# A macaron block with fp32 matmuls by splits: sums of weights issued after the next splits, the first gate block copied out of its banks, the first norm's squares spread out, the plain block's pass scheduled later

## The chip, the core and the metric

The kernel runs on one core of a Trainium2 chip. The metric is the device time of one execution in microseconds. The engines are TensorE (PE: matmuls, with PEld for its weight loads), VectorE (DVE), ScalarE (ACT), GpSimd (POOL) and SyncE (SP, which here issues loads only).

## The reference, cut to what matters

256 tokens of width 2048 pass a half-step feed-forward, two mixers merged by gates, a second half-step feed-forward and a last norm. All data are float32.

```python
x = x + 0.5 * swiglu_ffn(rmsnorm(x, norm_ffn1_g), ffn1_w_gate, ffn1_w_up, ffn1_w_down)
h = rmsnorm(x, norm_mix_g)
proj = h @ w_in                       # 2048 x 11264: q, k, v, retention q, k, v, g, two gates
att = chunked_band_attention(...)     # 8 heads
ret = silu(g_r) * chunkwise_retention(rotary(q_r), rotary(k_r), v_r)
merged = sigmoid(gate_a) * (att @ w_out_att) + sigmoid(gate_r) * (ret @ w_out_ret)
x = x + merged @ w_out
x = x + 0.5 * swiglu_ffn(rmsnorm(x, norm_ffn2_g), ffn2_w_gate, ffn2_w_up, ffn2_w_down)
return rmsnorm(x, norm_final_g)

def swiglu_ffn(x, w_gate, w_up, w_down):      # 2048 -> 5632 -> 2048
    return (silu(x @ w_gate) * (x @ w_up)) @ w_down
```

## The kernel before, in words

**Products by splits.** A float32 product is made of three passes of a reduced format: every weight tile (128 x 2 x 512, two slices of the contraction) is split into a high half `hi` (a rounding copy on ScalarE, L129) and a low half `lo` (the difference, on VectorE, L130). `three` (L135 to L143) then issues hi times hi (L140), lo of the activations times hi (L141), and hi times lo of the weights (L143). The matmuls of L143 are the ones that need VectorE's `lo`.

**Steps.** All work of TensorE is a list `steps`, written out in order before anything is issued. A *standard* step multiplies one weight tile with both halves of the tokens: twelve matmuls. A step of a group (below) has six. `prep` of a step issues its split; `products` issues its matmuls. `run` goes through the list: at step c it first calls `prep_upto`, which issues the splits up to three steps ahead (four pairs of split tiles, `SPLIT_BUFS`), then the functions that are due at step c (`due`, filled by `later` and `at`), then the products of step c. Within an engine instructions run in the order in which they were issued.

**Groups.** Pairs of 512-column blocks, a gate block with its up block or two gate blocks of the mixer, are computed by a scheme of the Strassen kind: seven half products instead of eight, at the price of sums of weight tiles on VectorE. A group has four phases; r steps use weights as loaded, s steps use sums, and each kind has four steps per phase, numbered 0 to 3 (0r0, 0r1, 0s0, 0r2, 0s1, 0r3, 0s2, 0s3, then phases 1 and 2 alike, then 3s0 to 3s3). A group's tiles bear its first step's number: z10 is the first group of the first feed-forward, followed by z46, z82, up to z334; z392 to z543 are the mixer's five; z692, z728, z765, up to z1018 are those of the second feed-forward. The sums: in phase 0 `first` (L532) adds the kept tile to x behind the split of an r step (for steps 0 and 1 in the feed-forwards, where steps 2 and 3 are added by a transfer, `ADDED`; for all four in the mixer); in phase 1 the raw tile is added (L594) behind the split of an r step, and `third` (L580, L581) takes a difference and issues an accumulating load on POOL behind the split of an s step. 0s0 splits the x that `first` made for 0r0, and so on.

**Weaving.** `weave` puts standard steps of other jobs between the pairs of a group's steps, by shares. In a feed-forward these are the *plain* block's gate and up products (block 10, not in a group), and the passes of the down projection: first block 10's pass, then those of blocks 0 to 9. `at_hand` says from which step on a pass may come: for the plain block six steps after its up product ends. `put_mid` transposes and splits the activations of a block four steps after it is done.

**The start.** The first ten steps are the gate block of the plain pair (steps 0 to 7) and the first two of its up block. The group z10 follows from step 10. The gate block uses two banks of tag "z", of which there are three and which the groups use too; its Silu is put off by `GATE_WAIT` = 5 steps until the first norm is known, whose eight squares are issued two at a time at steps 8 to 11. Close by lie the sums of the normed activations (L486 to L500). At the end of the up product, `close` seeds the banks of the next pass (L791) around `up_done` (L758), which multiplies up with the gate.

Of the kernel before, what the change touches and what calls it, by code (L numbers as in the profile page):

```python
# [10 lines left out]
AF = mybir.ActivationFunctionType  # L11
# [4 lines left out]
P = 128  # L16
SEQ = 256
NT = SEQ // P
D = 2048
# [7 lines left out]
NB = 512  # L27
# [19 lines left out]
ADDED = (2, 3)  # L47
PLAIN = 10
PASSES = ((10,),) + tuple((b,) for b in range(10))
GATE_WAIT = 5  # L50
WARM = (6, 3)
TAIL_PARTS = ((0, slice(0, NB)), (1, slice(0, NB // 2)), (1, slice(NB // 2, NB)))

# [22 lines left out]
def block_kernel(ctx: ExitStack, tc: tile.TileContext, x, g1, w1g, w1u, w1d, gm, w_in, rel, woa, wor, wo,  # L76
                 g2, w2g, w2u, w2d, gf, cos, sin, decay, ident, out):
    nc = tc.nc
# [19 lines left out]
    def tmp_tile(name, tag="t", bufs=None):  # L98
        return tmp.tile([P, NB], F32, tag=tag, name=name, bufs=bufs)


    steps = []
    transfers = []
    kept = []
    state = {"dma": 0, "kept": 0, "prep": 0, "step": 0, "slots": SPLIT_BUFS}
    room = {"raw": RAW_BUFS, "kept": KEPT}
    due = {}

    def later(n, fn):
        due.setdefault(state["step"] + n, []).append(fn)  # L110

    def weights_tile(name):
        return wpool.tile([P, KC, NB], F32, tag="raw", bufs=RAW_BUFS, name=name)
# [111 lines left out]
    def load_some():  # L225
        while state["dma"] < len(transfers) and room["raw"]:
            room["raw"] -= 1
            transfers[state["dma"]]()
            state["dma"] += 1
        while state["kept"] < len(kept) and room["kept"] > 0 and kept[state["kept"]][0] <= state["step"]:  # L230
            room["kept"] -= 1
            kept[state["kept"]][1]()
            state["kept"] += 1

    def prep_upto(n):

        while state["prep"] < min(len(steps), n) and state["slots"]:
            s = steps[state["prep"]]
            load_some()
            state["slots"] -= 1  # L240
            s.prep()
            for ring in s.frees:
                room[ring] += 1
            state["prep"] += 1
        load_some()
# [270 lines left out]
    class Strassen:  # L516
# [50 lines left out]
        def step(self, phase, jc, of_sum):  # L567
            made = {}
            name = f"{self.name}{phase}{jc}{'rs'[of_sum]}"
            n = HALF_K // KC  # L570

            def load():
                made["raw"] = weights_tile(f"raw{name}")
                i = 2 - phase
                fetch(made["raw"], self.w[i], self.rows(1, jc), self.col[i])

            def third():

                x, k = self.x[jc], self.kept[jc]
                nc.vector.tensor_sub(k, x, k)  # L580
                nc.gpsimd.dma_start(x, chunk(self.w[0], self.rows(1, jc), self.col[0]), accum_op=ALU.add)  # L581

            def prep():
                x = self.x[jc]
                if not of_sum:
                    if phase == 0:
                        made["w"] = split(self.kept[jc], name)
                        if jc not in self.added:
                            self.first(jc)
                        return  # L590
                    raw = made.pop("raw")
                    made["w"] = split(raw, name)
                    if phase == 1:
                        nc.vector.tensor_add(x, x, raw)  # L594
                elif phase == 2:
                    made["w"] = split(self.kept.pop(jc), name)
                elif phase == 3:
                    made["w"] = split(self.x.pop(jc), name)
                else:
                    made["w"] = split(x, name)  # L600
                    if phase == 1:
                        third()

            bank, form, fresh, closing = {
# [4 lines left out]
            }[phase, of_sum]  # L609

            def products():
                hi, lo = made["w"]
                if fresh and jc == 0:
                    self.bank(bank)
                three([
                    (
                        self.acc[bank], self.norm.form(form, KC * jc + i), (hi[:, i, :], lo[:, i, :]),
                        fresh and jc == 0 and i == 0, closing and jc == n - 1 and i == KC - 1,
                    )
                    for i in range(KC)  # L620
                ], True)
                if jc == n - 1:
                    self.end(phase, of_sum)

            loaded = not of_sum and phase in (1, 2)
            frees = ["raw"] if loaded else ["kept"] if of_sum and phase > 1 else []
            return Step(self, 0, load if loaded else None, prep, frees, products)

        def end(self, phase, of_sum):
# [51 lines left out]
    def weave(jobs, apart, groups, lead, share, start=None, extra=0):  # L681


        queue = [(job, k) for job in jobs for k in range(0, job.nk, KC)]
        at_hand = {}

        def next_standard():

            if len(queue) <= apart:
                return False  # L690
            job, k = queue[0]
            if any(at_hand.get(b, len(steps) + 1) > len(steps) for b in job.needs):
                return False
            steps.append(standard(job, k))
            del queue[0]
            if job.makes is not None and k + KC == job.nk:
                at_hand[job.makes] = len(steps) + 6
            return True

        for _ in range(lead):  # L700
            next_standard()
        ends = []
        rate = (len(queue) - apart) / (len(groups) * sum(share))
        credit = 0.0
        first = max(len(steps) - 8, D // NB)
        for n, (b, make) in enumerate(groups.items()):
            group = make()
            loads = group.loads()
            if start is not None and n == 0:
                loads[0] = lambda load=loads[0]: [start(), load()]  # L710
            kept.extend((first + i if n == 0 else 0, fn) for i, fn in enumerate(loads))
            for i, part in enumerate(group.steps()):
                steps.extend(part)
                credit += rate * share[i]
                if i + 1 == len(share):
                    at_hand[b] = len(steps) + 7

                turn = i + 1 == 3 * (HALF_K // KC)
                if (turn or credit >= (0.2 if (i + 1) % (HALF_K // KC) == 0 else 0.6)) and next_standard():
                    credit -= 1  # L720
            ends.append(len(steps))
        if extra:
            due.setdefault(ends[0], []).append(lambda: room.update(kept=room["kept"] + extra))
            due.setdefault(ends[-1], []).append(lambda: room.update(kept=room["kept"] - extra))
        for job, k in queue:
            steps.append(standard(job, k))

    def ffn(name, norm, wg, wu, wd, after, start=None):
# [10 lines left out]
        def plain(b):  # L739
            gates = {}  # L740

            wait = GATE_WAIT if start is not None and b == PLAIN else 0

            def gate_done(acc):
                def go():
                    for t in range(NT):
                        gates[t] = tmp_tile(f"{name}g{b}{t}", "gate", 2)
                        nc.scalar.activation(gates[t], acc[t], AF.Silu, scale=norm.scale(t))

                if wait:  # L750
                    later(wait, go)
                else:
                    go()

            def up_done(acc):
                for t in range(NT):
                    a = gates[t]
                    nc.vector.scalar_tensor_tensor(a, acc[t], norm.scale(t), a, op0=ALU.mult, op1=ALU.mult)  # L758
                later(4, lambda: put_mid(b, gates))

            tags = ("acc", "acc")
            up = Gemm(wu, 0, b * NB, D // P, norm, up_done, tags)
            up.makes = b
            return [Gemm(wg, 0, b * NB, D // P, norm, gate_done, ("z", "z") if wait else tags), up]

        def paired(b):
            got = {}
# [46 lines left out]
    n1 = Norm("n1", gains[:, 0, :], True)  # L814
# [13 lines left out]
    scale = HD ** -0.5  # L828
# [316 lines left out]
    def at(step, fn):  # L1145
        due.setdefault(step, []).append(fn)
# [40 lines left out]

    for c in range(2, 2 * (D // NB)):
        at(c - 1, lambda c=c: n1.put(c // 2, c % 2))
    for b in range(D // NB):  # L1190
        at(D // NB * 2 + b, lambda b=b: [n1.square(b, t) for t in range(NT)])
    at(60, load_angles)

    def set_bias():
# [77 lines left out]
```

## Time and profile before

| | |
|---|---|
| median of 3 runs | 2061.39 us (2060.89 to 2062.56) |
| the profiled execution | 2061.97 us, its span 2060.1 us |
| mean granted TensorE clock | 0.998 |
| TensorE busy | 2037.8 us (99%), 9208 matmuls |
| VectorE busy | 1766.2 us (86%) |
| ScalarE busy | 1494.1 us (73%) |
| POOL busy | 344.8 us (17%) |
| bytes moved | 498.47 MB, mean 242 GB/s |

A row of the timeline reads: start, duration (both us), engine, line, operation, output <- inputs, shapes, count, and in brackets the idle time before it with what ended that. A row of the list of waits reads: who waited, for whom, us in total, how often, the longest. Names such as loz29801r mean: the low half for group z298, phase 0, tile 1, an r step. Durations of neighbouring rows overlap a little, since an instruction starts before the one ahead of it has fully ended; times from start to start are what an engine needs for each.

### The profile page before, as it was taken

The page shows a single profiled execution, that of the slowest core. Times are in us where ns is not written, and L with a number is a line of the kernel's source. Part 1 is how long each engine was busy: PE and PEld are TensorE (multiplying, and loading weights), DVE is VectorE, ACT ScalarE, POOL GpSimd, SP SyncE. Part 2 cuts the span into 40 slices and gives each one's busy share as a digit, 9 for nine tenths or more (in the row PEclk, how much of TensorE's full clock was granted, in tenths as well). Part 3 has the DMA queues.
Part 4 walks back from the last instruction along what each step waited for, and adds up shares of the span by engine and source line. Part 5 has one row for each costly group of instructions (what it writes and reads, how often), then busy time and mean ns, then how long its engine had stood idle before and what let it go on. Part 6 is the DMA issues. An engine that isn't in the chain of part 4 may idle for free.

```text
span 2060.1 us, 26318 instructions
## 1 busy us (share of the span) xinstructions
PE 2037.8 (99%) x9208; PEld 1685.6 (82%) x9208; DVE 1766.2 (86%) x1836; ACT 1494.1 (73%) x1892; POOL 344.8 (17%) x386
## 2 busy tenths in 40 slices
PE   9999999999999999999999999999999999999998
PEld 7888888888888888888888888888888888888886
DVE  7999999999999799889966667569989999989996
ACT  8778877887877767776765434556788888887875
POOL 2221222221222110121100000012122212112200
PEclk9999999999999999999999999999999999999999
DMA  9888899888888677898786645578889888889983
GB/s 308 252 232 260 252 274 273 254 229 252 254 250 244 241 206 262 263 288 240 228 277 184 216 142 189 185 231 218 267 267 278 255 255 234 269 261 268 276 214 133
DMA packets 230325, 498.47 MB, mean 242 GB/s; under 512 B 15584, under 2 KB 16336, under 8 KB 230192
## 3 DMA queue, kind: packets, MB, share of 16 engines
q1 hardware_dynamic: 156736, 301.50, 43.5%
q0 software_dynamic: 70112, 189.44, 36.0%
q10 hardware_dynamic: 3344, 5.84, 0.8%
q8 instruction: 72, 1.18, 0.2%
q14 instruction: 61, 0.50, 0.1%
HBM read 487.81 MB, written 8.91 MB: 241 GB/s over the span
## 4 chain that ended last, share of the span: by engine, by line
PE 92%; ACT 3%; DVE 3%; issue 1%; DMA 1%; DVEq 0%; ACTq 0%; POOLq 0%; POOL 0%
PE acc L143 15%; PE acc L140 15%; PE acc L141 15%; DVE lo L130 1%; DMA raw<-in_w_in_dram 1%; ACT hi L129 0%; PE z392a L143 0%; PE z873a L140 0%; PE z910a L141 0%; PE z765a L141 0%; PE z543a L143 0%; PE z430a L143 0%; PE z801a L143 0%; PE z392a L141 0%; PE z505a L143 0%
## 5 line engine op out<-in xcount | busy, mean ns | idle before, releaser
L130 DVE TENSOR_TENSOR lo<-raw,hi 128x1024 fp32r<-128x1024 f32 x367 | 447.1, 1221 | 142.6 <-ACT hi L129 140.8
L129 ACT CAST hi<-raw 128x1024 fp32r<-128x1024 f32 x367 | 384.3, 1051 | 173.3 <-PE acc L141 138.0
L794 ACT ACTIVATE xall<-acc 128x512 f32<-128x512 f32 x160 | 94.5, 591 | 14.5 <-PE acc L143 10.3
L791 ACT ACTIVATE acc<-xall 128x512 f32<-128x512 f32 x160 | 95.8, 599 | 8.2 <-DVE f1g L758 4.3
L140 PE MATMUL acc<-hi,mgh 128*128 128x512 f32 x128 | 50.2, 392 | 0.0
L141 PE MATMUL acc<-hi,mgl 128*128 128x512 f32 x128 | 49.8, 389 | 0.0
L140 PE MATMUL acc<-hi,nma01h 128*128 128x512 f32 x96 | 38.8, 404 | 0.1
L140 PE MATMUL acc<-hi,nma00h 128*128 128x512 f32 x96 | 38.6, 402 | 0.0
L141 PE MATMUL acc<-hi,nma00l 128*128 128x512 f32 x96 | 37.5, 390 | 0.0
L141 PE MATMUL acc<-hi,nma01l 128*128 128x512 f32 x96 | 37.5, 390 | 0.0
L140 PE MATMUL acc<-hi,nma10h 128*128 128x512 f32 x96 | 37.5, 390 | 0.0
L141 PE MATMUL acc<-hi,nma11l 128*128 128x512 f32 x96 | 37.4, 390 | 0.0
L140 PE MATMUL acc<-hi,nma11h 128*128 128x512 f32 x96 | 37.4, 390 | 0.0
L141 PE MATMUL acc<-hi,nma10l 128*128 128x512 f32 x96 | 37.4, 390 | 0.0
L143 PE MATMUL acc<-lo,mgh 128*128 128x512 f32 x128 | 35.5, 389 | 0.0
L143 PE MATMUL acc<-lo,nma01h 128*128 128x512 f32 x96 | 29.6, 390 | 0.0
L143 PE MATMUL acc<-lo,nma11h 128*128 128x512 f32 x96 | 29.6, 389 | 0.0
L143 PE MATMUL acc<-lo,nma00h 128*128 128x512 f32 x96 | 29.6, 389 | 0.0
L143 PE MATMUL acc<-lo,nma10h 128*128 128x512 f32 x96 | 29.6, 389 | 0.0
L143 PEld LDWEIGHTS acc<-lo,mgh 128*128 128x128 f32 x128 | 24.0, 188 | 5.0
L141 PEld LDWEIGHTS acc<-hi,mgl 128*128 128x128 f32 x128 | 24.0, 188 | 4.9
L140 PEld LDWEIGHTS acc<-hi,mgh 128*128 128x128 f32 x128 | 24.0, 188 | 4.8
(6634 smaller groups left out, 7134.3 us busy)
## 6 DMA issues: line engine op xcount, KB each, us to landing
raw<-in_ffn_w_down_dram SPq DMA_DIRECT2D x176, 512.0 KB, 7.6
raw<-in_w_in_dram SPq DMA_DIRECT2D x96, 512.0 KB, 4.7
raw<-in_w_out_dram SPq DMA_DIRECT2D x32, 512.0 KB, 4.1
raw<-in_ffn_w_up_dram SPq DMA_DIRECT2D x16, 512.0 KB, 6.4
raw<-in_w_out_att_dram SPq DMA_DIRECT2D x16, 512.0 KB, 4.3
raw<-in_w_out_ret_dram SPq DMA_DIRECT2D x16, 512.0 KB, 3.9
raw<-in_ffn_w_gate_dram SPq DMA_DIRECT2D x15, 512.0 KB, 4.8
z392x<-in_w_in_dram POOLq DMA_DIRECT2D x8, 512.0 KB, 7.5
```

Source lines behind the costliest of these rows:

```text
L129: nc.scalar.copy(hi, raw)
L130: nc.vector.tensor_sub(lo, raw, hi.bitcast(F32))
L140: nc.tensor.matmul(acc, ahi, whi, start=first, stop=False, **more)
L141: nc.tensor.matmul(acc, alo, whi, start=False, stop=False, **more)
L143: nc.tensor.matmul(acc, ahi, wlo, start=False, stop=last, **more)
L791: nc.scalar.activation(acc, xs[t][:, cols], AF.Copy, scale=2.0)
L794: nc.scalar.activation(xs[t][:, cols], acc, AF.Copy, scale=0.5)
```

## The change

- The sums are put off: `soon(n, fn)` keeps a function until n further splits have been issued. `first` and the phase 1 addition of r steps go behind the next split, `third` behind the second next. The raw tile of a phase 1 r step is counted as free only when its addition has been issued.
- The plain block's pass may come nine steps after its up product instead of six. Written out, the list of steps changes in two groups only. In z10 the two standard steps of that pass leave phase 2 (behind 2r2 and 2s3) and stand behind 2s3 and 3s2. In z728 the phase 0 order 0r0, 0r1, standard, 0s0, 0r2, standard, 0s1, 0r3, 0s2, 0s3, standard becomes 0r0, 0r1, 0s0, 0r2, 0s1, 0r3, standard, 0s2, 0s3, standard, and phases 1 and 2 are shifted by one standard step.
- The first gate block uses the banks of tag "acc"; ScalarE copies it unscaled into two tiles of another ring when it is done, and the Silu, with the norm's scale, runs on these in place, twelve steps later.
- The eight squares of the first norm are issued one at a step at steps 10 to 17.

```diff
-GATE_WAIT = 5
+GATE_WAIT = 12
+SQUARES = 10
...
+    postponed = []
+
+    def soon(n, fn):
+        postponed.append([n, fn])
...
             load_some()
             state["slots"] -= 1
+            waiting = list(postponed)
             s.prep()
+            for p in waiting:
+                p[0] -= 1
+                if p[0] == 0:
+                    p[1]()
+                    postponed.remove(p)
             for ring in s.frees:
                 room[ring] += 1
...
                         if jc not in self.added:
-                            self.first(jc)
+                            soon(1, lambda: self.first(jc))
                         return
                     raw = made.pop("raw")
                     made["w"] = split(raw, name)
                     if phase == 1:
-                        nc.vector.tensor_add(x, x, raw)
+
+                        def second():
+                            nc.vector.tensor_add(x, x, raw)
+                            room["raw"] += 1
+
+                        soon(1, second)
...
                     if phase == 1:
-                        third()
+                        soon(2, third)
...
-            frees = ["raw"] if loaded else ["kept"] if of_sum and phase > 1 else []
+            frees = ["raw"] if loaded and phase == 2 else ["kept"] if of_sum and phase > 1 else []
...
             if job.makes is not None and k + KC == job.nk:
-                at_hand[job.makes] = len(steps) + 6
+                at_hand[job.makes] = len(steps) + 9
...
             def gate_done(acc):
-                def go():
+                for t in range(NT):
+                    gates[t] = tmp_tile(f"{name}g{b}{t}", *(("qk", 4) if wait else ("gate", 2)))
+
+                def go(srcs):
                     for t in range(NT):
-                        gates[t] = tmp_tile(f"{name}g{b}{t}", "gate", 2)
-                        nc.scalar.activation(gates[t], acc[t], AF.Silu, scale=norm.scale(t))
+                        nc.scalar.activation(gates[t], srcs[t], AF.Silu, scale=norm.scale(t))
 
                 if wait:
-                    later(wait, go)
+                    for t in range(NT):
+                        nc.scalar.copy(gates[t], acc[t])
+                    later(wait, lambda: go(gates))
                 else:
-                    go()
+                    go(acc)
...
-            return [Gemm(wg, 0, b * NB, D // P, norm, gate_done, ("z", "z") if wait else tags), up]
+            return [Gemm(wg, 0, b * NB, D // P, norm, gate_done, tags), up]
...
-    for b in range(D // NB):
-        at(D // NB * 2 + b, lambda b=b: [n1.square(b, t) for t in range(NT)])
+    for i in range(NT * D // NB):
+        at(SQUARES + i, lambda i=i: n1.square(i // NT, i % NT))
```

## The prediction

> **What bounds the kernel now.** I read the busy times of the page first, then the list of TensorE's waits, then the timeline around each of these waits and around the same places where nothing waits.
>
> ```profile
> PE 2037.8 (99%) x9208; PEld 1685.6 (82%) x9208; DVE 1766.2 (86%) x1836; ACT 1494.1 (73%) x1892; POOL 344.8 (17%) x386
> ...
> L130 DVE TENSOR_TENSOR lo<-raw,hi 128x1024 fp32r<-128x1024 f32 x367 | 447.1, 1221 | 142.6 <-ACT hi L129 140.8
> ```
>
> TensorE is the bound at 99%, VectorE stands close behind at 86%. So only TensorE's waits can be won, and an edit that makes VectorE late anywhere is paid in full.
>
> ```profile
> PE acc L143 <- DVE lo L130: 4.9, 9, 0.6
> PE z10c L140 <- ACT f1g L748: 2.2, 1, 2.2
> PE acc L141 <- DVE f2a10l L380: 1.4, 1, 1.4
> ...
> PE z1018c L143 <- DVE loz101800s L130: 0.6, 1, 0.6
> PE z982c L143 <- DVE loz98200s L130: 0.5, 1, 0.5
> ...
> PE acc L141 <- DVE f1a10l L380: 0.5, 1, 0.5
> ```
>
> These are what the change aims at: a low half that comes late in nine group starts of the first feed-forward and two of the second (z982, z1018), the bank of the gate block (z10c), and the plain block's pass (f1a10, f2a10). All other group starts of the second feed-forward and of the mixer wait for nothing now, so they can only lose.
>
> **Part 1: the sums put off, where a standard step follows.** The steps of a first-feed-forward group begin 0r0, 0r1, standard, 0s0 (r: kept weights, s: the sums). The timeline of group z298:
>
> ```profile
> 534.97 1.22 DVE L130 TENSOR_TENSOR loz29800r<-z298k,hiz29800r 128x1024 fp32r<-128x1024 f32 x1
> 535.63 1.04 ACT L129 CAST hiz29801r<-z298k 128x1024 fp32r<-128x1024 f32 x1
> 536.11 1.22 DVE L532 TENSOR_TENSOR z298x<-z298x,z298k 128x1024 f32<-128x1024 f32 x1
> ...
> 539.14 0.39 PE L140 MATMUL acc<-hi,f1a6h 128*128 128x512 f32 x1
> 539.51 1.22 DVE L130 TENSOR_TENSOR lo<-raw,hi 128x1024 fp32r<-128x1024 f32 x1
> 540.79 0.73 PE L143 MATMUL acc<-lo,f1a6h 128*128 128x512 f32 x2 [0.58 <-DVE lo L130]
> 541.36 0.40 PE L140 MATMUL acc<-hi,f1a6h 128*128 128x512 f32 x1
> ```
>
> VectorE runs lo r0, sum 0, lo r1, sum 1, lo standard, each 1.13 us behind the last (534.97, 536.11). Six matmuls take 1.36 us at 0.227 from start to start; from 539.14 to 541.36 they took 2.22, so the wait costs 0.86, more than its 0.58. After the change the order is lo r0, lo r1, sum 0, lo standard, sum 1, lo s0. Lo r1 now stands directly behind lo r0, but its high half is only there at 535.63 + 1.04 = 536.67: lo r1 starts at 536.72, the sum at 537.86, lo standard at 538.99 instead of 539.51. Gain 0.52, not 0.86. Lo s0 then ends near 542.5, some 0.5 before it is needed, so no new wait. Eight groups (z82 to z334): -4.2 us, between -6.9 (all 0.86) and 0.
>
> **Part 1 where no standard step follows.** Seven of the later groups begin 0r0, 0r1, 0s0, 0r2. The timeline of z801, which does not wait now:
>
> ```profile
> 1579.83 1.22 DVE L130 TENSOR_TENSOR loz80100r<-z801k,hiz80100r 128x1024 fp32r<-128x1024 f32 x1
> 1580.49 1.04 ACT L129 CAST hiz80101r<-z801k 128x1024 fp32r<-128x1024 f32 x1
> 1580.97 1.22 DVE L532 TENSOR_TENSOR z801x<-z801x,z801k 128x1024 f32<-128x1024 f32 x1
> 1582.30 1.06 ACT L129 CAST hiz80100s<-z801x 128x1024 fp32r<-128x1024 f32 x1 [0.77 <-DVE z801x L532]
> 1584.37 1.22 DVE L130 TENSOR_TENSOR loz80100s<-z801x,hiz80100s 128x1024 fp32r<-128x1024 f32 x1
> 1585.51 1.22 DVE L130 TENSOR_TENSOR loz80102r<-z801k,hiz80102r 128x1024 fp32r<-128x1024 f32 x1
> 1586.32 0.61 PE L143 MATMUL z801c<-loz80100s,n2s5h 128*128 128x512 f32 x2
> 1587.68 0.62 PE L143 MATMUL z801a<-loz80102r,n2a00h 128*128 128x512 f32 x2
> ```
>
> Step s0 splits the sum itself: its high half on ScalarE waits for sum 0 (the row at 1582.30), its low half for that. Now sum 1 fills this time on VectorE. After the change sum 0 starts behind lo r1: high half of r1 ends 1581.53, lo r1 1581.57, sum 0 1582.7 to 1583.9, high half of s0 1584.0 to 1585.1, lo s0 1585.15, and VectorE stands still for 1.2 us because sum 1 is queued behind lo s0. Then sum 1 at 1586.3, lo r2 at 1587.4 to 1588.6 instead of 1585.51. TensorE wants it with its weight load 0.23 before 1587.68: some 1.2 us late, and no later wait takes that back. z837 has the same rows (+1.2). In z765 sum 1 delays the last combination that the next transposes need, by the same 1.13 (+1.25). In z910 and z946 a standard step between the groups leaves room: 0. In z982 (z1018 alike) there is nothing in hand:
>
> ```profile
> 1888.28 1.04 ACT L129 CAST hiz98201r<-z982k 128x1024 fp32r<-128x1024 f32 x1
> 1892.17 1.22 DVE L130 TENSOR_TENSOR loz98200s<-z982x,hiz98200s 128x1024 fp32r<-128x1024 f32 x1
> 1894.93 0.62 PE L143 MATMUL z982a<-loz98202r,n2a00h 128*128 128x512 f32 x2
> ```
>
> The same walk from 1889.36 (lo r1) gives lo s0 at 1892.9 and lo r2 done at 1896.4, against 1894.70 for its weight load: +1.7 each, so the 0.5 us waits grow to over 2.
>
> The mixer's z430 has this order too, and sums in all four steps:
>
> ```profile
> 790.90 1.05 ACT L129 CAST hiz43001r<-z430k 128x1024 fp32r<-128x1024 f32 x1 [0.45 <-ACT z392c L1041]
> 797.62 0.62 PE L143 MATMUL z430a<-loz43002r,nma00h 128*128 128x512 f32 x2
> ```
>
> Lo r1 at 792.0, sum 0 to 794.35, lo s0 795.55, lo r2 done at 799.05 against 797.4: +1.6; z392 (r3 and s3 without a standard step between) +0.3, z543 +0.1. Mixer together +2.0, between 0 and +3.
>
> **Part 1 in the second phase.** Every sum there follows its split one or two places later, but standard steps lie between, so each low half has as many or fewer instructions ahead of it than now: 0. The raw buffer comes free one VectorE instruction (1.13 us) later, and SP's next load with it; POOL's accumulating loads shift by two to three. A whole phase of eight steps (eight times 1.36 us) hides both; if it did not, a late raw tile would stop ScalarE's split and cost its lateness in full.
>
> **Part 2: the plain block's pass, three steps later.** In the first feed-forward the pass goes to the end of phase 2; that is in part 3's sum. In the second, group z728 loses its first standard step and becomes 0r0, 0r1, 0s0, 0r2, 0s1, 0r3.
>
> ```profile
> 1455.52 1.04 ACT L129 CAST hiz72801r<-z728k 128x1024 fp32r<-128x1024 f32 x1
> ```
>
> The f2a10l wait goes (1.7 with its restart). But the walk from 1456.6 gives the high half of s0 at 1460.05 for a step due at 1459.5, and behind lo s0 (to 1461.3), sum 1 and two low halves of the plain block, lo r2 ends at 1464.8, 2.2 us late. Ahead of the pass the steps stand some 1.5 us later than now: +1.5, between -1.7 (the wait goes, nothing comes) and +3.
>
> **Part 3: the gate block, the squares, the first group.**
>
> ```profile
> 33.82 1.06 ACT L129 CAST hiz1001r<-z10k 128x1024 fp32r<-128x1024 f32 x1 [1.38 <-PE acc L141]
> 34.91 1.23 DVE L130 TENSOR_TENSOR loz1001r<-z10k,hiz1001r 128x1024 fp32r<-128x1024 f32 x1 [0.22 <-ACT hiz1001r L129]
> 47.31 0.50 PE L140 MATMUL z10c<-hiz1000s,n1s5h 128*128 128x512 f32 x1 [2.19 <-ACT f1g L748]
> 47.95 0.63 PE L140 MATMUL z10c<-hiz1000s,n1s5h 128*128 128x512 f32 x1
> 48.38 0.63 PE L141 MATMUL z10c<-hiz1000s,n1s5l 128*128 128x512 f32 x1
> 54.74 0.57 ACT L634 COPY z10b<-z10a 128x512 f32<-128x512 f32 x1 [0.77 <-PE z10a L143]
> ...
> 78.82 1.22 DVE L580 TENSOR_TENSOR z10k<-z10x,z10k 128x1024 f32<-128x1024 f32 x1
> 81.09 1.40 DVE L758 SCALAR_TENSOR_TENSOR f1g<-acc,n1rstd,f1g 128x512 f32<-128x512 f32 x2
> 81.87 0.60 ACT L791 ACTIVATE acc<-xall 128x512 f32<-128x512 f32 x1 [4.29 <-DVE f1g L758]
> ```
>
> And VectorE's busy time in two stretches, from the first sum to phase 1 and from there to the end of the f1g product:
>
> ```profile
> 34.00:57.77 23.77, 20.83 (x27) 0.93 0.73 213
> 57.77:82.49 24.72, 24.72 (x23) 1.00 0.84 223
> ```
>
> The z10c wait goes: 2.3 us and 1.7 more, since the next nine matmuls start 0.43 apart (47.95, 48.38; the granted clock of that stretch is 0.93) instead of 0.227. Two copies of 0.57 (the price of row 54.74) come in; the second delays the split of 33.82 by about 1. Lo r1 starts at 35.9 instead of 34.91, with sum 0 still behind it: VectorE is 2.1 us back. It was idle for 2.9 us in the first stretch, so it only just catches up by the start of phase 1; in the second stretch it was never idle. TensorE comes 4 us early and has to wait for it. Squares, table load and Silu, now near 57 to 60, hold ScalarE another 0.5 to 1 us. One put-off difference (as at 78.82) passes behind the f1g product, which so ends near 81.9, 0.6 earlier; the transposes and the second half of phase 2 hang on it. There eight steps without a standard one ask for VectorE every 1.36 us while it has the put-off difference, two low halves and a combination to fit in. I get the start of z46 about 1 us later than now, less its own 0.86 wait that the late pass removes: +0.1 instead of -5.6, between -4 and +2.
>
> **Sum.** -4.2 + 2.0 + (1.25 + 1.2 + 1.2 + 1.7 + 1.7) + 1.5 + 0.1 = +6.4 us. The profiled execution took 2061.97 us (span 2060.1), 0.6 above the median 2061.39 of the runs; on the median this is 2067.8, 0.3% slower.
>
> **Rivals.**
> The clock falls at the new waits. Row 47.31: a wait of 2.19 halved the rate of nine matmuls (1.7 us); the f2a10l wait of 1.4 did not, since the span lost there was the wait alone. My longest new waits are 2.2 (z728) and 1.6 (ahead of the f1a10 transposes). If two of them pay, 2071.2.
> [...]
> The first group keeps its 4 us, VectorE catching up where I see it bound: 2063.7, no change. For it: the 2.9 us of gaps before phase 1, which more than the 2.1 could fill; against: none from there to 82.49.
> Faster: the waits go and nothing comes. That is 4.0 (z10c) + 0.7 (f1a10) + 9 x 0.86 + 2 x 0.84 + 1.7 = 15.8 us: 2045.6. It is decided by one thing, whether s0's high half still starts before TensorE needs it; it would hold if ScalarE had r1's high half at least 1.2 us earlier. Row 1582.30, a split that waits for the sum already, speaks against it. With half of that gain and half of my costs (10.5) it is -7.9 + 5.3: 2058.8, the low end of the range.
>
> **How the numbers follow.** About 0.2% (4.1 us) is what a measurement here can tell from none. My sum 0.48 (2065 to 2071), the clock falling as well 0.12, the first group's gain kept 0.26, faster 0.14. Slower 0.60, same 0.26, faster 0.14. The range 2058 to 2073 leaves out most of the last case and the far end of the second.
>
> **What would show it.** Right: the L143 wait of the f1 starts at 0.1 to 0.3 instead of 0.58; ScalarE's s0 split in z801 waiting for L532 until about 3.5 us behind r1's split, and TensorE waiting for lo of 0r2 there and in z837, z982, z1018, z430; the z10c wait gone, but the f1a10 transposes still near 82. Wrong: z801 to z837 without a wait, or f1a10 transposes at 80.

## The result, and the profile after

The changed kernel takes 2076.41 us (median of 4 runs, 2074.92 to 2077.41) against 2061.14 before: a ratio of 1.0072 (95% interval 1.006 to 1.0084), 15.3 us slower where +6.4 was forecast. Its profiled execution has a span of 2075.1 us, 15.0 more, at the same mean clock of 0.998. The diff moves line numbers: L129, L130 and L140 to L143 of before are L134, L135 and L145 to L148 here, `first` is L543, the second sum L607, `third` L591 and L592.

The busy times and the chain of work that ended last, from the page of after:

```profile
PE 2048.4 (99%) x9208; PEld 1681.8 (81%) x9208; DVE 1769.9 (85%) x1836; ACT 1476.0 (71%) x1894; POOL 344.5 (17%) x386
...
PE 80%; DMA 6%; ACT 5%; issue 4%; DVE 4%; POOL 1%; ACTq 0%; DVEq 0%; POOLq 0%
PE acc L145 14%; PE acc L146 14%; PE acc L148 14%; DMA z190x<-in_ffn_w_gate_dram 1%; DMA z837x<-in_ffn_w_gate_dram 1%; ACT hi L134 1%; DMA z154x<-in_ffn_w_gate_dram 1%; DMA z298x<-in_ffn_w_gate_dram 1%; DMA z801k<-in_ffn_w_up_dram 1%; DMA z46x<-in_ffn_w_up_dram 0%; DMA z298x<-in_ffn_w_up_dram 0%; DVE lo L135 0%; ACT xall L814 0%; DMA z46k<-in_ffn_w_up_dram 0%; DMA z154x<-in_ffn_w_up_dram 0%
```

The same shares in the page of before:

```profile
PE 92%; ACT 3%; DVE 3%; issue 1%; DMA 1%; DVEq 0%; ACTq 0%; POOLq 0%; POOL 0%
```

TensorE is still "busy" for 99%, which tells nothing. The chain does: transfers (DMA) hold 6% of it, where they held 1%, and the largest of these are x tiles of groups of the feed-forwards. The list of TensorE's waits of after, the two waits of the start and of the mixer's norm left out:

```profile
PE z10c L145 <- ACT z10s L653: 2.7, 1, 2.7
PE z728a L148 <- DVE loz72802r L135: 1.6, 1, 1.6
...
PE z298c L145 <- ACT z298s L653: 1.0, 1, 1.0
...
PE z1018c L145 <- ACT hiz101800s L134: 0.9, 1, 0.9
PE z982c L145 <- ACT hiz98200s L134: 0.9, 1, 0.9
...
PE z801a L148 <- DVE loz80102r L135: 0.6, 1, 0.6
PE z837a L148 <- DVE loz83702r L135: 0.6, 1, 0.6
...
PE z430a L148 <- DVE loz43002r L135: 0.6, 1, 0.6
```

The row "acc <- lo, 9 times" of before is gone, and z728, z801, z837, z982, z1018 and z430 wait for the low halves that the prediction named (z982 and z1018 also for the high half of 0s0). Two kinds of row it did not have: z10c waiting 2.7 us for ScalarE's L653, and the same line in z298 (and, at 0.2 to 0.5, in z46, z118, z154 and z190). L653 is ScalarE's scaled copy of bank c; step 1r0 writes into bank c again and must wait for it.

Where the time went is read best by the start of each group. The table gives the start of a group's first matmul in the timeline of a kernel, less its start in before (us; the last column is step 3s3 of z1018). Column to column it shows the first group, the first feed-forward's groups, the mixer, z728, and the rest.

| kernel | z46 | z392 | z692 | z765 | z873 | end |
|---|---|---|---|---|---|---|
| changed | +1.0 | +5.4 | +7.1 | +8.7 | +11.8 | +15.1 |
| e1 first sums alone | -0.2 | -5.0 | -2.3 | -0.1 | +3.0 | +6.2 |
| e2 second sums alone | -0.1 | +1.0 | +3.1 | +3.1 | +3.1 | +3.0 |
| e3 third sums alone | -0.9 | +7.5 | +7.0 | +7.0 | +7.0 | +10.5 |
| e4 gate block and squares alone | -1.9 | -1.6 | -2.1 | -2.1 | -2.1 | -2.1 |
| e5 changed, third sums at once | +0.9 | -4.2 | +0.4 | +1.9 | +5.0 | +8.2 |
| e6 e3 with early loads | -0.4 | -0.3 | -0.7 | -0.8 | -0.8 | -0.8 |
| e7 later pass alone | +0.9 | 0.0 | -0.4 | -0.8 | -0.8 | -0.8 |
| e10 changed with early loads | +1.1 | -4.1 | -2.0 | -0.5 | +2.6 | +5.8 |

Each row is one profiled execution: that of e2 was 1.5 us slower than the median of its runs, that of e5 1.9 faster. The profiled execution of before lost 0.4 us in the mixer's z467, where a raw tile came late; all kernels but e2 and e5 are without that loss, so in their rows 0.4 us of what stands from z692 on is not an effect of the edit.

As an example of the rows behind the table, the first matmul of z298 in before, after and e10, in this order:

```profile
536.42 0.39 PE L140 MATMUL z298a<-hiz29800r,n1a00h 128*128 128x512 f32 x1
```

```profile
539.92 0.39 PE L145 MATMUL z298a<-hiz29800r,n1a00h 128*128 128x512 f32 x1
```

```profile
533.38 0.39 PE L145 MATMUL z298a<-hiz29800r,n1a00h 128*128 128x512 f32 x1
```

The changed kernel loses 4.4 us between z46 and z392, where the prediction had it win 4.2. The rest of the table's first row is near the forecast. So there was one thing to find: what the nine groups of the first feed-forward pay.

**The chain behind it in z298.** POOL's loads for z298, first in before, then in after (L581 and L592: the accumulating loads that `third` issues; L543 and L554: tiles of the next group; L547 and L558: the accumulate onto two of its x tiles; in brackets the idle time ahead):

```profile
515.01 1.20 POOL L581 DMA_DIRECT2D z262x<-in_ffn_w_up_dram  x1 [1.54 <-ACT hiz26221r L129]
...
521.77 0.73 POOL L543 DMA_DIRECT2D z298x<-in_ffn_w_gate_dram  x1 [1.90 <-DVE loz26221s L130]
533.49 1.23 POOL L547 DMA_DIRECT2D z298x<-in_ffn_w_up_dram  x1 [10.98 <-DMA z298x<-in_ffn_w_gate_dram]
537.40 1.21 POOL L547 DMA_DIRECT2D z298x<-in_ffn_w_up_dram  x1 [2.68 <-DMA z298x<-in_ffn_w_gate_dram]
...
547.48 1.06 ACT L129 CAST hiz29803s<-z298x 128x1024 fp32r<-128x1024 f32 x1 [0.30 <-PE z298c L141]
```

```profile
522.48 1.20 POOL L592 DMA_DIRECT2D z262x<-in_ffn_w_up_dram  x1 [2.19 <-ACT hiz26220s L134]
...
525.41 1.20 POOL L554 DMA_DIRECT2D z298x<-in_ffn_w_gate_dram  x1
...
526.96 1.08 POOL L554 DMA_DIRECT2D z298x<-in_ffn_w_gate_dram  x1
541.37 1.24 POOL L558 DMA_DIRECT2D z298x<-in_ffn_w_up_dram  x1 [13.32 <-DMA z298x<-in_ffn_w_gate_dram]
544.83 1.22 POOL L558 DMA_DIRECT2D z298x<-in_ffn_w_up_dram  x1 [2.23 <-DMA z298x<-in_ffn_w_gate_dram]
...
554.19 1.05 ACT L134 CAST hiz29803s<-z298x 128x1024 fp32r<-128x1024 f32 x1 [4.09 <-DMA z298x<-in_ffn_w_up_dram]
...
560.65 0.69 ACT L653 ACTIVATE z298s<-z298c,n1minus 128x512 f32<-128x512 f32 x1
561.39 0.50 PE L145 MATMUL z298c<-hiz29810r,n1s3h 128*128 128x512 f32 x1 [1.01 <-ACT z298s L653]
```

Read each against the start of z298 (536.42 and 539.92). The last accumulating load of z262 goes out 21.4 us ahead of it before, 17.4 after: 4.0 later. Six loads of z298 stand behind it on POOL. By the trace's times of landing they come in one behind the other, 1.6 to 2.1 us apart in both kernels, so the last of them, which goes out 13.0 us ahead of the start instead of 14.7, lands 4.6 behind it instead of 0.7. The accumulate onto the fourth x tile must wait until that tile has landed, and is issued 4.9 us behind the start instead of 1.0. From issue to landing it then takes 9.3 us instead of 6.2, so that its data are there 14.2 us behind the start instead of 7.2. In before the split of 0s3 came 11.1 us behind the start: the data had been there for 3.9 us, and its wait of 0.30 was for a free split tile. In after it waits 4.09 us for the data, everything behind it on ScalarE is late, L653 too, and TensorE waits at 1r0.

That is about half of the loss. By steps, the nine groups from z46 to z334 of after win 5.2 us at their starts, between 0r0 and 0s3, as e5 and e10 do. Then they lose 4.4 between 0s3 and 1s3, nearly all of it at 1r0 and 1r1, and 5.2 more in phase 2, at waits too short for the list. In z298 the second part shows at 2r1: the low half on VectorE and TensorE's matmul with it in after, then the low half in e10, whose start is 533.38.

```profile
584.48 1.22 DVE L135 TENSOR_TENSOR loz29821r<-rawz29821r,hiz29821r 128x1024 fp32r<-128x1024 f32 x1
585.75 0.73 PE L148 MATMUL z298b<-loz29821r,n1a01h 128*128 128x512 f32 x2
```

```profile
575.03 1.22 DVE L135 TENSOR_TENSOR loz29821r<-rawz29821r,hiz29821r 128x1024 fp32r<-128x1024 f32 x1
```

Against the start of z298 this low half begins at 44.6 us in after and at 41.7 in e10, with the same order of sums. VectorE had to wait for the late high half of 0s3 too and has been 2.9 us behind since, while TensorE has lost only 1.4 by then; so the low half comes late for it, 0.3 us at 2r1 and again at 2r3. Why z82 loses nothing and z262 only 0.4 stays open.

**The first group.** ScalarE and TensorE of after around 1r0 of z10, then TensorE at the same place in the best version (e8):

```profile
56.84 1.05 ACT L134 CAST hiz1011r<-rawz1011r 128x1024 fp32r<-128x1024 f32 x1
57.90 1.28 ACT L766 ACT_TABLE_LOAD   x1
59.20 1.33 ACT L766 ACTIVATE f1g<-f1g,n1rstd 128x512 f32<-128x512 f32 x2
60.44 0.67 ACT L653 ACTIVATE z10s<-z10c,n1minus 128x512 f32<-128x512 f32 x1
...
61.16 0.80 PE L145 MATMUL z10c<-hiz1010r,n1s3h 128*128 128x512 f32 x1 [2.67 <-ACT z10s L653]
61.75 0.63 PE L146 MATMUL z10c<-hiz1010r,n1s3l 128*128 128x512 f32 x1
62.18 0.63 PE L145 MATMUL z10c<-hiz1010r,n1s3h 128*128 128x512 f32 x1
```

```profile
60.47 0.50 PE L145 MATMUL z10c<-hiz1010r,n1s3h 128*128 128x512 f32 x1 [2.67 <-ACT z10s L651]
60.81 0.39 PE L146 MATMUL z10c<-hiz1010r,n1s3l 128*128 128x512 f32 x1
61.04 0.40 PE L145 MATMUL z10c<-hiz1010r,n1s3h 128*128 128x512 f32 x1
```

The bank wait of before is gone and z10 runs 4.3 us early from 0s1 on. But the put-off Silu with its table load stands directly ahead of L653 on ScalarE: 2.54 us from 57.90 to 60.44, and TensorE waits 2.67. Behind that wait the next matmuls of after start 0.43 apart instead of 0.23, so that of the 4.3 us 1.5 are left at 1r0 and 0.1 at 1r1. The busy times and the granted clock (third from the right) of after in the two stretches that the prediction quoted show the slow clock moved from one to the other:

```profile
34.00:57.77 23.77, 23.77 (x107) 19.68 (x106) 21.20 (x27) 20.93 (x36) 3.19 (x3) 1.00 0.75 204
57.77:82.49 24.72, 22.05 (x91) 17.79 (x90) 23.33 (x22) 15.32 (x18) 3.61 (x3) 0.93 0.77 207
```

### The profile page after: what moved, and what is told of

It reads as the page before. It is cut to its first block, busy times and chain, and to the rows that moved or that the text cites. A ratio compares the mean times of both kernels' runs of the same rounds, so it can differ in the third digit from the quotient of the medians.

```text
span 2075.1 us, 26299 instructions
## 1 busy us (share of the span) xinstructions
PE 2048.4 (99%) x9208; PEld 1681.8 (81%) x9208; DVE 1769.9 (85%) x1836; ACT 1476.0 (71%) x1894; POOL 344.5 (17%) x386
## 4 chain that ended last, share of the span: by engine, by line
PE 80%; DMA 6%; ACT 5%; issue 4%; DVE 4%; POOL 1%; ACTq 0%; DVEq 0%; POOLq 0%
PE acc L145 14%; PE acc L146 14%; PE acc L148 14%; DMA z190x<-in_ffn_w_gate_dram 1%; DMA z837x<-in_ffn_w_gate_dram 1%; ACT hi L134 1%; DMA z154x<-in_ffn_w_gate_dram 1%; DMA z298x<-in_ffn_w_gate_dram 1%; DMA z801k<-in_ffn_w_up_dram 1%; DMA z46x<-in_ffn_w_up_dram 0%; DMA z298x<-in_ffn_w_up_dram 0%; DVE lo L135 0%; ACT xall L814 0%; DMA z46k<-in_ffn_w_up_dram 0%; DMA z154x<-in_ffn_w_up_dram 0%
## 5 line engine op out<-in xcount | busy, mean ns | idle before, releaser
L135 DVE TENSOR_TENSOR lo<-raw,hi 128x1024 fp32r<-128x1024 f32 x367 | 446.5, 1220 | 136.8 <-ACT hi L134 134.7
L134 ACT CAST hi<-raw 128x1024 fp32r<-128x1024 f32 x367 | 383.3, 1049 | 162.9 <-PE acc L146 135.1
L145 PE MATMUL acc<-hi,mgh 128*128 128x512 f32 x128 | 50.2, 392 | 0.0
L145 PE MATMUL acc<-hi,nma01h 128*128 128x512 f32 x96 | 38.6, 403 | 0.0
L145 PE MATMUL acc<-hi,nma00h 128*128 128x512 f32 x96 | 38.6, 402 | 0.0
L145 PE MATMUL acc<-hi,nma11h 128*128 128x512 f32 x96 | 37.4, 390 | 0.0
L145 PE MATMUL acc<-hi,nma10h 128*128 128x512 f32 x96 | 37.4, 390 | 0.0
L148 PE MATMUL acc<-lo,mgh 128*128 128x512 f32 x128 | 35.5, 389 | 0.0
L148 PE MATMUL acc<-lo,nma00h 128*128 128x512 f32 x96 | 29.6, 390 | 0.0
L148 PE MATMUL acc<-lo,nma01h 128*128 128x512 f32 x96 | 29.6, 390 | 0.0
L148 PE MATMUL acc<-lo,nma11h 128*128 128x512 f32 x96 | 29.6, 389 | 0.0
L148 PE MATMUL acc<-lo,nma10h 128*128 128x512 f32 x96 | 29.6, 389 | 0.0
L148 PEld LDWEIGHTS acc<-lo,mgh 128*128 128x128 f32 x128 | 24.0, 188 | 5.0
L145 PEld LDWEIGHTS acc<-hi,mgh 128*128 128x128 f32 x128 | 24.0, 188 | 4.9
```

Source lines behind the costliest of these rows:

```text
L134: nc.scalar.copy(hi, raw)
L135: nc.vector.tensor_sub(lo, raw, hi.bitcast(F32))
L145: nc.tensor.matmul(acc, ahi, whi, start=first, stop=False, **more)
L148: nc.tensor.matmul(acc, ahi, wlo, start=False, stop=last, **more)
```

## The experiments

The theory (A in the expectations): the loss inside the first feed-forward's groups comes from the put-off second and third sums, through late loads on POOL and late splits on ScalarE. Rivals: the first sums start it (B), first and second sums together make it (C), or VectorE's changed order does, not the loads (D). The helper `soon` and its call in `prep_upto`, as in the diff of the change, belong to e1, e2, e3 and e6 as well and are not shown again. Ratios are to the kernel before, in runs of the same chip.

**e1, the first sums alone.** 

```diff
-                            self.first(jc)
+                            soon(1, lambda: self.first(jc))
```

> The kernel before with one part of the change alone: only the first sum of a group's weights is put off behind the next split. Theory A (the loss inside the first feed-forward's groups comes from the second and third sums, through ScalarE's split of the sum and through POOL's accumulating load): this part keeps its eight starts of 0.52 us (-4.2) and pays the mixer (+1.7) and z765, z801, z837, z982 and z1018 (+6.3): +3.8 us in all, 2065. Rival B (the put-off first sum itself starts the loss inside the groups): z82 to z392 loses some 4 us as in the changed kernel instead of gaining 4, and the whole is +12 us, 2073.

2068.12 us, 1.0033 (1.002 to 1.0045). Between z46 and z392 it wins 4.8 us, 0.5 to 0.6 at each of nine starts, and nothing is lost inside a group: B falls. It loses 2.7 in the mixer, 6.3 from z765 on, and, which I had not expected of it, 2.2 at z728. There TensorE's wait for f2a10l, the low half of the plain block's activations, grows from 1.39 to 1.97 us, and behind it the granted clock (third from the right in the second row) falls to 0.68, where before has 1.00 over the 5.40 us from the same matmul on:

```profile
1459.59 0.50 PE L145 MATMUL acc<-hi,f2a10l 128*128 128x512 f32 x1 [1.97 <-DVE f2a10l L390]
```

```profile
1459.60:1465.00 5.40, 5.40 (x17) 4.28 (x18) 5.40 (x6) 1.23 (x3) 1.49 (x2) 0.68 1.01 198
```

The changed kernel does not have this wait; its later pass takes it away. The walk of the prediction for z801 can be read in after's timeline nearly to the digit:

```profile
1590.10 1.03 ACT L134 CAST hiz80101r<-z801k 128x1024 fp32r<-128x1024 f32 x1
1593.64 1.05 ACT L134 CAST hiz80100s<-z801x 128x1024 fp32r<-128x1024 f32 x1 [2.50 <-DVE z801x L543]
...
1594.72 1.22 DVE L135 TENSOR_TENSOR loz80100s<-z801x,hiz80100s 128x1024 fp32r<-128x1024 f32 x1 [1.20 <-ACT hiz80100s L134]
1595.87 1.22 DVE L543 TENSOR_TENSOR z801x<-z801x,z801k 128x1024 f32<-128x1024 f32 x1
1597.00 1.22 DVE L135 TENSOR_TENSOR loz80102r<-z801k,hiz80102r 128x1024 fp32r<-128x1024 f32 x1
```

ScalarE's split of 0s0 stands 3.54 us behind that of 0r1 (forecast 3.5), VectorE stands still for 1.20 us (forecast 1.2) with the second sum queued behind the instruction that waits.

**e2, the second sums alone.**

```diff
-                        nc.vector.tensor_add(x, x, raw)
+                        def second():
+                            nc.vector.tensor_add(x, x, raw)
+                            room["raw"] += 1
+                        soon(1, second)
...
-            frees = ["raw"] if loaded else ["kept"] if of_sum and phase > 1 else []
+            frees = ["raw"] if loaded and phase == 2 else ["kept"] if of_sum and phase > 1 else []
```

> The kernel before with only the second sum put off behind the next split, its raw buffer freed one split later. Theory A: ScalarE's fast half of the split of the sum at 1s3 waits some 3 to 4 us for the sum, and TensorE then loses about 0.3 us at 2s0 and 0.3 us at 2s2 of each of the nine groups of the first feed-forward: +5 us, 2066. Rival B (the first sum is the cause, or all three together are needed): no change within 1 us, 2061.

2063.49 us, 1.0011 (1.0002 to 1.002). My own account of it fell: no group of the first feed-forward after z46 loses anything. The two losses are 1.0 in z46 and 2.0 in the mixer's z467, where TensorE waits 1.9 for a split of a raw tile that came late. Its runs spread from 2062.07 to 2065.71, those of before on the same chip from 2060.37 to 2062.14. That the raw tile's buffer, freed one split later, makes that load late is likely and was not tried.

**e3, the third sums alone.**

```diff
-                        third()
+                        soon(2, third)
```

> The kernel before with only the third sums put off by two splits. Theory A: POOL's last accumulating load of each pair goes out some 4 us later, the next group's kept weights stand behind it on POOL, the accumulate into the first of them lands late, and TensorE waits at 1r0 for ScalarE's copy of bank c by 0 to 1 us in each of nine groups: +3 us, 2064 (if the first and second sums must be late too, less: 0 to +1). Rival B (the loads have a whole phase of cover): no change, 2061.

2072.01 us, 1.005 (1.0037 to 1.0062): 10.8 us, much more than either theory gave it, and the largest of the five parts. Every group from z46 to z334 loses 0.6 to 1.6, z1018 3.5, all of it from 0s3 to 1s0 and nothing in phase 2.

**e6, the third sums with the next group's loads earlier.** POOL may run four tiles ahead instead of two, so only four loads of the next group, not six, stand behind the last accumulating load.

```diff
-EXTRA = 2
+EXTRA = 4
```

> The third sums put off as in the run of that part alone, but four extra tiles granted to POOL's queue in place of two, so that the second pair of the next group's tiles is loaded ahead of the previous group's accumulating loads (order on POOL alone, nothing else moved). Theory A (the late part is the load of the next group's x tiles behind the last accumulating load, and the accumulate onto them): hi of 0s3 no longer waits for its tile, and of the 10.8 us that this part cost the 7 us in the first feed-forward's groups come back: 2063 to 2065. Rival D (the loss comes from VectorE's order, the sums standing later among its splits, and not from the loads): 2071 to 2072, as that part alone.

2061.01 us, 1.0001 (0.9992 to 1.001): the whole 10.8 us come back, more than expected, since those of z1018 come too, with the sums as late on VectorE as in e3. D falls; it is the loads. The row of ScalarE's split of 0s3 of z298 in e3, then in e6:

```profile
555.51 1.05 ACT L133 CAST hiz29803s<-z298x 128x1024 fp32r<-128x1024 f32 x1 [3.17 <-DMA z298x<-in_ffn_w_up_dram]
```

```profile
547.26 1.06 ACT L133 CAST hiz29803s<-z298x 128x1024 fp32r<-128x1024 f32 x1 [0.30 <-PE z298c L145]
```

**e10, the same edit in the full change.**

> The changed kernel with nothing undone but four extra tiles granted to POOL's queue in place of two, so that more of the next group's tiles are loaded ahead of the previous group's put-off accumulating loads. Theory A (in the full change too the first feed-forward loses by those loads): as much comes back as when the third sums are issued at once, 4 to 7 us: 2070 to 2072. Rival (with all three sums put off ScalarE's late split of the sum at 1s3 alone still holds the groups): under 2 us come back, 2075.

2068.01 us, 1.0035 (1.0022 to 1.0048), 8.4 below the changed kernel, more than expected; nothing else was undone. Behind the starts the groups from z46 to z334 lose nothing, in phase 2 neither. POOL and ScalarE at z298, to be read against its start at 533.38:

```profile
519.52 0.73 POOL L554 DMA_DIRECT2D z298x<-in_ffn_w_gate_dram  x1 [1.54 <-DVE loz26221s L135]
...
533.16 1.21 POOL L558 DMA_DIRECT2D z298x<-in_ffn_w_up_dram  x1 [2.64 <-DMA z298x<-in_ffn_w_gate_dram]
...
543.90 1.06 ACT L134 CAST hiz29803s<-z298x 128x1024 fp32r<-128x1024 f32 x1 [0.30 <-PE z298c L146]
```

The row at 519.52 is the fourth and last load behind the accumulating ones. It lands 0.5 us ahead of the group's start where the sixth landed 4.6 behind it; two loads of some 2 us each are gone from the queue. The second accumulate is issued 0.2 us ahead of the start instead of 4.9 behind it, and the split waits for a free split tile again.

**e5, the changed kernel with the third sums issued at once** (the edit of e3 taken back).

> The changed kernel with one part undone: the third sums are issued at once, as before. Theory A (the put-off third sums are what the first feed-forward's groups lose by): the starts won by the first sums come through, z392 starts some 5 us earlier than in the kernel before instead of 5.4 later, and the wait at z1018's 1r0 goes: about 2066 us, 10 below the changed kernel. Rival C (first and second sums together make the same loss, by ScalarE's late split at 1s3): at most 3 us of it, 2073.

2072.12 us, 1.0053 (1.0041 to 1.0066). The total misses the 2066: it is 4.3 below the changed kernel, not 10, and by itself would stand nearer to C. The groups decide. From z46 to z334 nothing is lost behind the starts, z392 starts 4.2 early, and rival C falls. The total is high partly because z467 loses 1.7 to a late raw tile; that place differs from kernel to kernel (e10, with the second sums put off too, loses nothing there), and the runs spread over 3.3 us. What decides it stays open. The wait of ScalarE's split of 1s3 for the second sum, which I had first blamed, is there in e5 as well, 2.26 us against 3.84 in after, and costs nothing:

```profile
567.54 1.05 ACT L134 CAST hiz29813s<-z298x 128x1024 fp32r<-128x1024 f32 x1 [2.26 <-DVE z298x L607]
```

**e4, the gate block and the squares alone** (the gate's banks, copies, GATE_WAIT = 12 and SQUARES = 10 of the diff).

> The kernel before with only the gate block's change: both blocks in the accumulators' banks, the first copied out unscaled, its Silu 12 steps on, and the first norm's squares one a step. Theory A: the group z10 starts 4 us earlier and loses nearly all of it at 1r0, where TensorE waits some 2.7 us for ScalarE's copy of bank c and runs at a slower clock behind that wait: -0.5 us in all, 2060.5. Rival B (the wait at 1r0 is there only because the put-off sums make VectorE and ScalarE late): the 4 us stay, 2057.

2060.39 us, 0.9997 (0.9988 to 1.0006). Between the two: z10 is 4.6 early, waits 1.54 us at 1r0 without a fall of the clock (1.00 from 58.16 to 80.41 us), and 1.9 are left at the start of z46. So the wait is there without any put-off sum, and the put-off first sums make it longer (2.67 in e8).

**e7, the plain block's pass alone** (6 to 9 in `at_hand`).

> The kernel before with only the pass over the plain block three steps later. Theory: it costs nothing on its own in the first feed-forward and takes away the wait at f2a10's transposes in the second (1.4 us): -1 us, 2060. Rival: the moved pass takes a standard step from z728's start and costs 1.5 us there, 2062.5.

2060.87 us, 0.9999 (0.999 to 1.0008): no change that can be told. In the first feed-forward it gives and takes back 0.9, at z728 it gains 0.4.

**e8, the parts that win, put together**: the edit of e4, and the first sums put off only where `self.norm is n1`, that is in the first feed-forward.

> The kernel before with the gate block's change and with the first sum put off in the first feed-forward's groups alone (the mixer's and the second feed-forward's sums, the second and third sums and the pass as before). Both parts were measured by themselves: starts -5.0 us up to z392, gate and squares -2.1 us. If they add, -7 us: 2054 us, ratio 0.9966. If the put-off first sum delays the group z10 or the gate's copies, the gate's part is lost: 2056.

2056.15 us, 0.9978 (0.9969 to 0.9987): 4.9 us below before on the medians and 20 below the changed kernel, 2 short of the sum of its parts; by the two profiled spans (2053.6 and 2060.1) it is 6.5. z46 is 1.1 early instead of 1.9, z392 6.1 early, and from there on nothing is lost. Its list of waits begins with the 2.7 us of z10c.

**e9, the Silu behind the copy of bank c** (e8 with GATE_WAIT = 16).

> As the version with the gate block's change and the first sums put off in the first feed-forward alone, with the copied gate's Silu 16 steps on in place of 12, which puts it and its table load behind ScalarE's copy of bank c instead of directly ahead of it. Theory A (the wait of 2.7 us at z10's 1r0 is that table load and Silu, 1.28 + 1.33 us): the wait goes and the group keeps its whole gain, 2 to 2.8 us more: 2053.6, ratio 0.9962. Rival (squares and splits ahead of it make ScalarE late anyway, or the Silu now delays a later split): no gain, 2056.

2056.92 us, 0.9978 (0.9969 to 0.9987): no gain. The 2.7 us wait is gone, as A said, and z10 is still 4.5 early at 1r0; but at its end only 0.8 are left. Busy times of e9 from the first sum of phase 1 on (TensorE, weight loads, VectorE, ScalarE, POOL):

```profile
58.16:80.41 22.25, 21.20 (x88) 16.08 (x88) 22.25 (x22) 12.98 (x14) 4.20 (x4) 1.00 0.82 226
```

VectorE is busy for all of the 22.25 us: it is the bound of that stretch, and TensorE falls back to its pace although the Silu, off ScalarE's way to bank c, no longer holds it up.

**e11, both** (e9 with EXTRA = 4).

> The kernel of the run with the Silu 16 steps on, and four extra tiles for POOL's queue. In the run of the third sums with early loads the added tiles gave -0.2 to -0.8 us against the kernel before in a kernel that had a use for them; here no accumulating load is late, so no change against that kernel, within 0.5 us.

2056.42 us, 0.9976 (0.9967 to 0.9985), as expected no more than e9. So the added tiles by themselves give nothing that can be told; what they brought back in e6 and e10 was the cost of the late loads.

## Why the prediction was right or wrong

In e10, the change with the loads out of the way, the prediction's sum can be held term by term against the table; the changed kernel stands beside it. By the medians e10 is 6.7 slower than before, by the profiled executions 5.8.

| term | forecast | e10 | changed |
|---|---|---|---|
| first group, up to z46's 0s0 | +0.1 | +0.2 | +0.1 |
| first feed-forward's groups | -4.2 | -4.3 | +5.3 |
| mixer | +2.0 | +2.1 | +1.8 |
| z728 and the pass | +1.5 | +1.5 | +1.5 |
| z765, z801, z837 | +3.65 | +3.1 | +3.1 |
| z982, z1018 | +3.4 | +3.2 | +3.3 |
| sum | +6.4 | +5.8 | +15.1 |

The step that failed is "Part 1 in the second phase". It named the right thing ("POOL's accumulating loads shift by two to three") and costed it at 0 because "a whole phase of eight steps" hides it. That cover was for the raw tiles and for the accumulating loads' own data; what POOL issues behind them was not followed. The next group's tiles stand there, with an accumulate onto them that can only go out some 16 to 18 us later, when they have landed (in after's rows of POOL from 525.41 to 541.37 and from 526.96 to 544.83). Its data had 3.9 us in hand before ScalarE's split of 0s3 read them, not the 10.9 of a phase, and they came 7.0 us later: 3.9 by the issue, 3.1 by the longer way to landing. The split's lateness then passed to TensorE at 1r0 and, by VectorE, in phase 2. The term measured 9.6 us in the full change (from -4.3 to +5.3), 10.8 alone (e3).

The other parts, by their own steps. The starts of the first feed-forward: right, in size (0.5 to 0.6 each, no 0.86) and in cause. The groups without a standard step: right, within 0.4 each. The mixer: the sum is right partly by luck. z392 lost 0.9 (changed) and 1.3 (e10) instead of 0.3, z430 1.2 instead of 1.6, and the 0.4 at z467 is no effect of the change. z728: right, in its waits too; in the changed kernel TensorE waits 0.5 us for the high half of 0s0 (0.55 by the walk) and 1.6 for the low half of 0r2 (2.2), and the wait for f2a10l is gone. It takes both parts: the later pass alone gains 0.4 there (e7), and the put-off first sums alone lose 2.2 by another wait (e1). The first group: the net is right, the way to it wrong. I had the gain last into phase 1 and end on VectorE; in the change it ended at 1r0, on a bank that ScalarE had not yet read, a dependency that I had not walked. The f1a10 transposes start at 83.17 us against 83.05 in before, not earlier, as forecast. VectorE is the second wall: in e9, without the wait at 1r0, most of the gain still ends on it.

Of the rivals, the clock did fall at a new wait, the one of 2.67 us that was not in my list (0.58 from 61.16 to 65.00 us); at the 1.60 of z728 it did not (1.00 from 1472.02 to 1476.50). "The first group keeps its 4 us" holds for 1.1 to 1.9 of them without the other parts. The faster side did not come, but e8 shows that a part of it was there to be had in the first feed-forward, where a standard step stands between 0r1 and 0s0.

## What to carry to other kernels

When an instruction that issues a transfer is moved, follow its queue, not its data: what stands behind it on that queue, when that lands, and how long after that its first reader comes now. That last time is what the move may use up: 3.9 us here, though the load had been issued 10.1 us ahead of its reader. A wait of the reader for something else does not tell it. And an edit that helps where one order of steps holds should be made there only; of the five parts only the first sums won clearly, and only in the first feed-forward; confined to it, and with the gate block's change, they give 0.9978.

## What the runs showed of the hardware

The clock's fall behind a wait does not follow the wait's length alone. The same wait of 2.19 us at the same matmul of z10 slowed the matmuls from the third on in before (0.43 from start to start, a granted clock of 0.59 from 47.31 to 51.50 us) and none in e3 (0.34 behind the first, then 0.23); of the waits of 2.67 us at 1r0, that of after slowed the very next matmul (0.59 behind the first, then 0.43), that of e8 none (0.34, then 0.23). Behind the wait of 1.97 at z728 in e1 the clock was 0.68 over 5.40 us, behind that of 1.39 at the same place in before 1.00 over as long. Behind the waits of 1.54 (e4) and 1.60 (z728 in after) it was 1.00. TensorE in e3 behind its 2.19 us:

```profile
46.91 0.50 PE L144 MATMUL z10c<-hiz1000s,n1s5h 128*128 128x512 f32 x1 [2.19 <-ACT f1g L758]
47.25 0.39 PE L145 MATMUL z10c<-hiz1000s,n1s5l 128*128 128x512 f32 x1
47.48 0.39 PE L144 MATMUL z10c<-hiz1000s,n1s5h 128*128 128x512 f32 x1
```

So falls came behind waits of 1.97, 2.19 and 2.67 us, but not behind every wait of 2.19 or 2.67, and the place where they began differs too. The 1.7 us that the prediction added to such a wait is a price that one profiled execution pays and another does not.

The table load ahead of the Silu takes 1.28 us in after, and 1.30 in all from its row at 57.90 to the Silu at 59.20; the split before it ended at 57.89. In before it takes 1.28 as well, and 1.30 from 45.27 to the Silu at 46.57, behind a split that ended at 45.25.
